# Key units of a paged attention in eight pairs, with a strip of queries for two sequences

## The chip, the cores and the metric

The kernel runs on one core of a Trainium2 chip. The metric is the device time of one execution in microseconds (us), smaller being better. A core has TensorE (PE in the profile; the loads of its stationary operand are listed apart as PEld), VectorE (DVE), ScalarE (ACT), GpSimd (POOL) and SyncE (SP). Each works through its own instructions in their order and waits on semaphores for the others. SP and POOL here also issue DMAs; all DMAs of the core share 16 DMA engines.

## The reference

One decoder layer: a half-step feed-forward block, a token mixer (a gated convolution beside a "forgetting" attention), a second half-step feed-forward block and a gated embedding. It is computed for 256 prompt tokens and for 8 sample sequences of 4 new tokens each, 288 columns in all. The change touches the attention of the sample group alone, whose past lies in pages of 128 rows:

```python
def fox_sample(q, k_new, v_new, logf_new, cache_k, cache_v, cache_logf, page_table):
    DB, T = q.shape[0], q.shape[1]                 # 8 sequences, 4 new tokens
    P = page_table.shape[1] * PAGE_SIZE            # 8 pages of 128 rows
    k_past = cache_k[page_table].reshape(DB, P, N_HEADS, HEAD_DIM)
    ...
    s = jnp.einsum('bqhd,bkhd->bhqk', q, k_all, preferred_element_type=jnp.float32) * SCALE
    s = s + Fq[..., None] - F[:, :, None, :]
    ...
    p = jax.nn.softmax(s, axis=-1)
    return jnp.einsum('bhqk,bkhd->bqhd', p.astype(v_all.dtype), v_all)
```

There are 64 pages of keys and 64 of values, 512 KB each (128 rows x 8 heads x 128 x 4 bytes).

## The kernel before, in words

**Layout.** Activations lie feature by token: 16 tiles of 128 features by 288 tokens. Every weight matrix is cut into chunks of 512 rows by 256 columns (512 KB), loaded by SP into eight slots (`wraw`, L237) and split by ACT and DVE into a high and a low fp32r part (`whi` L276, `wlo` L277, five half-chunks of buffer). A chunk is one step of the program, called a piece below: 2 output blocks x 4 row blocks x 3 matmuls (L313 to L315) = 24 matmuls of 128x128 by 128x288.

**The attention stage.** `pair()` gives lists of such pieces. After the queries' projection the rest of the mixer is one list `fill`: pieces 0 to 15 project the keys, 16 to 51 three of the four convolution groups, and so on. The table `marks` puts other work ahead of chosen pieces, by `at(i, ...)`; `between()` strings both together. So the order of TensorE is: pieces, and ahead of some of them a marked function.

**A key unit.** There are 16 units; unit n holds four pages (half a past) of one sequence. Its keys come by four indirect DMAs that POOL issues (L248) into a tile `KT` of 2 MB, of which there are two. Its scores are 8 matmuls (L688) of 128x32 by 128x512 in plain fp32, four at a time in four column strips of the array; the profile counts each as two, 16 rows in all. The 32 stationary columns are a window on a zeroed `strip` into which DVE copies the four queries of the sequence at columns 28 to 31 (L679); the window's place decides to which rows of the PSUM bank the queries go, so that four units add into one bank. After the fourth, DVE adds the bank to the score tile `s` (L694).

**Order.** Unit n stands ahead of piece 1 + 3n (`KSTEP` = 3): pieces 1, 4, ... 46. The loads of a unit are an item of the same look-ahead list as the weight chunks (`load_upto`, eight items ahead). A KT tile is free when the matmuls of the unit two before it are done; POOL waits for that in its own order. The new tokens' scores (`new_scores`, L703) stand ahead of piece 22, the two softmaxes (`softmax`, L712 to L716) ahead of 27 and 49, the start of the value stage (`v_start`) ahead of 48, and its first round (L746) ahead of 51. POOL also writes the eight key blocks of the result to memory (L614, 144 KB each), as they come out of pieces 0 to 15.

Of the kernel before, what the change touches and what calls it, by code (L numbers as in the profile page):

```python
# [16 lines left out]
F32 = mybir.dt.float32  # L17
# [3 lines left out]
ALU = mybir.AluOpType  # L21
# [4 lines left out]
P = 128  # L26
D = 2048
KT = D // P
# [6 lines left out]
NH = 8  # L35
CB = 8
PAGES = 8
# [7 lines left out]
HALVES = 5  # L45
MANUAL = False
BANKS = dict(mm=3, kt=3, va=2)
KSTEP = 3
WEIGHTS = 4
VPAGES = 3  # L50
AHEAD = 12
# [42 lines left out]
def build(nc, tc, ctx, A, O):  # L94
# [3 lines left out]
    v, s, g, pe, sy = nc.vector, nc.scalar, nc.gpsimd, nc.tensor, nc.sync  # L98
# [8 lines left out]
    def bank(tag, bufs):  # L107
        return ps.tile([P, 512], F32, name=tag, tag=tag, bufs=bufs)
# [15 lines left out]
    h = cst.tile([P, KT, NT], F32, name="h")  # L124
# [11 lines left out]
    at = 0  # L136
# [13 lines left out]
    idx = cst.tile([P, 64], I32, name="idx")  # L150
# [74 lines left out]
    steps = []  # L225
# [3 lines left out]
    def load_upto(n):  # L229
        while state["loaded"] < min(n, len(items)):  # L230
            it = items[state["loaded"]]
            if it["kind"] == "p" and "vx" not in W:
                return
            if it["kind"] == "w":
                state["wslot"] = (state["wslot"] + 1) % (WEIGHTS if state["pages"] and not state["through"] else RAW)
                t = rawp.tile([P, it["nk"], 256], F32, name="wraw", tag=f"raw{state['wslot']}")
                src = it["src"]  # L237
                if state["loaded"] == 0:
                    tc.keep_in_program_order(sy.dma_start(t[:, :2], src[:, :2]))
                    d = sy.dma_start(t[:, 2:], src[:, 2:])  # L240
                else:
                    d = sy.dma_start(t, src)
                if state["used"] < 24:
                    tc.keep_in_program_order(d)
            elif it["kind"] == "k":
                t = W["kt"][0].tile([P, 4, NH, P], F32, name="KT", tag="KT", bufs=2)
                for i, r in enumerate(it["rows"]):
                    g.indirect_dma_start(out=t[:, i].rearrange("p h s -> p (h s)"), out_offset=None, in_=it["src"],  # L248
                                         in_offset=bass.IndirectOffsetOnAxis(ap=r, axis=0))
            else:  # L250
                t = page_tile()
                g.indirect_dma_start(out=t, out_offset=None, in_=it["src"],  # L252
                                     in_offset=bass.IndirectOffsetOnAxis(ap=it["rows"], axis=0))
            it["tile"] = t
            state["loaded"] += 1

    def page_tile():

        own = ([(rawp, f"raw{i}") for i in range(WEIGHTS, RAW)] + [(W["vx"][0], f"v{i}") for i in range(VPAGES)]
               + [(W["mix"][0], "wideb")])  # L260
        n = state["pages"]
# [76 lines left out]
    def do(fn):  # L338
        steps.append(([], fn))
# [3 lines left out]
    def defer(fn, chunks=1):  # L343

        deferred.append((state["chunk"] + chunks, fn))
# [137 lines left out]
    M = {}  # L483
# [156 lines left out]
    def q_gather():  # L640

        kq = W["kq"][0]
        qs = M["qs"] = kq.tile([P, NH, NS], F32, name="qs")
        for hh in range(NH):
            v.tensor_copy(qs[:, hh, :], q[hh][:, SEQ:])
        M["strip"] = kq.tile([P, NH, 60], F32, name="strip")
        g.memset(M["strip"], 0.0)
        M["qn"] = []
        for gi in range(2):
            t = kq.tile([P, NH, 4, 2, DT], F32, name=f"qn{gi}")  # L650
            g.memset(t, 0.0)
            for hh in range(NH):
                v.tensor_copy(t[:, hh, :, hh // 4, :], qs[:, hh, 16 * gi:16 * gi + 16].rearrange("p (b t) -> p b t", t=DT))
            M["qn"].append(t.rearrange("p h b a t -> p h (b a t)"))

    def wide(pool_name, slot, name):
        return W[pool_name][0].tile([P, 9 * P], F32, name=name, tag=f"wide{slot}")

    def fb_load(gi):

        t = wide("mix", "ab"[gi], f"s{gi}")
        for c in range(4):
            off = FS.offset + (gi * 4 * NH + c) * PAGES * P
            g.dma_start(t[32 * c:32 * c + 32, :PAGES * P],
                        bass.AP(tensor=FS.tensor, offset=off,
                                ap=[[NH * PAGES * P, 4], [4 * PAGES * P, 2], [0, DT], [1, PAGES * P]]))
        M["s", gi] = t[:, :PAGES * P + NS]
        x = t[:, :PAGES * P]
        v.tensor_scalar(x, x, -1.0, M["Fq"][gi], ALU.mult, ALU.add)

    def k_scores(n):

        gi, pp, bb = n // 8, n // 4 % 2, n % 4
        seq = 4 * gi + bb
        it = dict(kind="k", src=A["cache_k"], rows=[idx[:, j:j + 1] for j in range(seq * PAGES + 4 * pp, seq * PAGES + 4 * pp + 4)])

        def fn():
            strip = M["strip"]
            v.tensor_copy(strip[:, :, 28:32], M["qs"][:, :, 4 * seq:4 * seq + 4])  # L679
            first, last = bb == 0, bb == 3  # L680
            if first:
                M["sb"] = bank("va", BANKS["va"])
            sb = M["sb"]
            for half in range(2):
                at = 28 - 8 * bb - 4 * half
                for c in range(4):
                    hh = 4 * half + c
                    pe.matmul(sb[32 * c:32 * c + 32, :], strip[:, hh, at:at + 32],  # L688
                              it["tile"][:, :, hh, :],
                              start=first and half == 0, stop=last and half == 1, tile_position=(0, 32 * c))  # L690
            if last:
                def add():
                    x = M["s", gi][:, pp * 512:pp * 512 + 512]
                    v.tensor_tensor(x, sb, x, ALU.add)  # L694

                defer(add, 0)
        return ([it], fn)
# [210 lines left out]
    def kv_start():  # L908
        closed("fp")
        for n in ("zq", "mix", "cv"):  # L910
            opened(n)
        opened("kq", "right")
        q_gather()
        fb_load(0)
        fb_load(1)

# [22 lines left out]
    do(mix_start)  # L939
    qe = qk_evac(q, 0, SCALE, "q")  # L940
    ke = qk_evac(k_, 8, None, "k")
    units = [k_scores(n) for n in range(16)]
    for i in range(4):
        steps.extend(pair(win, 3072 + i * 256, ks, xact, qe(i), **(dict(late=2, tag="va") if i == 0 else {})))
        if i < 2:
            steps.append((units[i][0], lambda: None))
# [14 lines left out]
    def out_conv(ob):  # L961
        def evac(b, o):
            k = 2 * ob + b
            t = W["cv"][0].tile([P, NT], F32, name="tB", tag="tB", bufs=3)
            v.tensor_tensor(t, o, rsc, ALU.mult)
            g.tensor_tensor(h[:, k, :], h[:, k, :], t, ALU.add)
        return evac
# [19 lines left out]
        fill += conv_pair(i)  # L987
    for ob in range(KT // 2):
        fill += pair(A["w_out"], ob * 256, list(range(8)), lambda k: zc[k], out_conv(ob), late=1 if ob == 0 else 0)
    for n in range(16):  # L990
        at(1 + KSTEP * n, units[n] if n > 1 else units[n][1])
    at(22, lambda: new_scores(0), lambda: new_scores(1))
    at(27, lambda: softmax(0))
    at(49, lambda: softmax(1))
    at(48, v_start)
# [152 lines left out]
```

## Time and profile before

| What | Value |
|---|---|
| median of 3 runs (lowest to highest) | 2330.11 us (2329.85 to 2330.43) |
| the profiled execution, its own time | 2329.32 us |
| its span, first to last instruction | 2327.5 us |
| granted TensorE clock | 0.998 |
| PE busy in the key stage, 910.8 to 1088.0 us | 177.2 of 177.2 us |
| DMA share and rate in the key stage | 0.87, 308 GB/s |
| DMA share and rate in the span before it, 0 to 840 us | 0.57, 178 GB/s |
| POOL busy in the key stage | 82.4 us |

The span leaves out about 1.8 us of the execution's time (2329.32 - 2327.5). The profile lists for each engine how long it was busy and, for each group of instructions, how long the engine was idle just before them and what ended that. The chain of waits goes back from the last instruction of the program to what released it, step by step; its rows give the start, the length and the line. A row of a stretch gives its busy time on each engine, the granted clock, the mean busy share of the 16 DMA engines and GB/s. A queue's row gives packets, MB and the share of the 16 engines' time; q0 is the queue of POOL's DMAs, q1 that of SP's.

### The profile page before, as it was taken

The numbers are of one execution on the slowest core, as the hardware profiler recorded it, in microseconds if no ns is written. First come the engines' busy times: TensorE is split into PE (matmuls) and PEld (weight loads), VectorE is DVE, ScalarE is ACT, GpSimd is POOL, SyncE is SP. The second block draws the span as 40 slices with busy tenths as digits, with TensorE's granted clock in tenths as the row PEclk, the third lists the DMA queues.
The fourth block names the chain that finished last, engine by engine and source line by source line (L and its number), as shares of the span: only waits on it lengthen the run. The fifth ranks groups of instructions, "written<-read, shape, count | busy, mean of one in ns | idle before, by whom it ended". The sixth has DMA issues, their size and how long they took to land.

```text
span 2327.5 us, 44281 instructions
## 1 busy us (share of the span) xinstructions
PE 2313.5 (99%) x17385; PEld 2253.7 (97%) x17385; DVE 1342.6 (58%) x2403; ACT 1058.9 (45%) x1865; POOL 330.6 (14%) x403
## 2 busy tenths in 40 slices
PE   9999999999999999999999999999999999999997
PEld 9999999999999999888888999999999999999997
DVE  7555555555555586456466765555555555555755
ACT  7444444444444453334344554444434444444654
POOL 2010000000000013444445210000000000000110
PEclk9999999999999999999999999999999999999999
DMA  8575555555555547987988555555555555555552
GB/s 272 161 242 163 164 168 164 167 163 164 166 167 166 163 159 228 333 314 268 320 317 294 164 165 158 176 154 173 164 167 164 167 163 164 165 167 166 165 166 88
DMA packets 341985, 443.43 MB, mean 191 GB/s; under 512 B 17120, under 2 KB 306288, under 8 KB 341776
## 3 DMA queue, kind: packets, MB, share of 16 engines
q1 hardware_dynamic: 320304, 366.81, 49.6%
q0 software_dynamic: 20384, 71.38, 9.0%
q8 instruction: 136, 2.23, 0.4%
q10 hardware_dynamic: 1088, 2.42, 0.3%
q14 instruction: 73, 0.60, 0.1%
HBM read 435.48 MB, written 5.07 MB: 189 GB/s over the span
## 4 chain that ended last, share of the span: by engine, by line
PE 99%; DVE 0%; ACT 0%; DMA 0%; issue 0%; DVEq 0%
PE mm L313 31%; PE mm L315 31%; PE mm L314 31%; PE va L688 1%; PE va L746 1%; PE va L315 1%; PE va L313 1%; PE va L314 1%; DVE h L1075 0%; PE kt L315 0%; PE kt L313 0%; PE kt L314 0%; DMA gT<-in_gains_dram 0%; PE kt L800 0%; PE kt L833 0%; PE kt L824 0%
## 5 line engine op out<-in xcount | busy, mean ns | idle before, releaser
L277 DVE TENSOR_TENSOR wlo<-wraw,whi 128x512 fp32r<-128x512 f32 x1384 | 973.8, 707 | 802.3 <-ACT whi L276 753.6
L276 ACT ACTIVATE whi<-wraw 128x512 fp32r<-128x512 f32 x1384 | 866.9, 630 | 933.0 <-PE mm L314 903.5
L313 PE MATMUL mm<-xh,whi 128*128 128x288 f32 x3680 | 1094.2, 297 | 0.0
L314 PE MATMUL mm<-xl,whi 128*128 128x288 f32 x3680 | 1085.7, 295 | 0.0
L315 PE MATMUL mm<-xh,wlo 128*128 128x288 f32 x3680 | 1082.0, 294 | 0.0
L313 PEld LDWEIGHTS mm<-xh,whi 128*128 128x128 f32 x3680 | 689.5, 187 | 22.2 <-issue 19.4
L315 PEld LDWEIGHTS mm<-xh,wlo 128*128 128x128 f32 x3680 | 693.0, 188 | 0.1
L314 PEld LDWEIGHTS mm<-xl,whi 128*128 128x128 f32 x3680 | 690.8, 188 | 0.1
L313 PE MATMUL mm<-hh,whi 128*128 128x288 f32 x1408 | 416.8, 296 | 0.0
L314 PE MATMUL mm<-hl,whi 128*128 128x288 f32 x1408 | 415.4, 295 | 0.0
L315 PE MATMUL mm<-hh,wlo 128*128 128x288 f32 x1408 | 414.0, 294 | 0.0
L379 POOL TENSOR_TENSOR sr<-sg,rs 128x288 f32<-128x288 f32 x88 | 72.5, 825 | 1408.9 <-ACT sg L377 1408.8
L315 PEld LDWEIGHTS mm<-hh,wlo 128*128 128x128 f32 x1408 | 265.2, 188 | 0.0
L314 PEld LDWEIGHTS mm<-hl,whi 128*128 128x128 f32 x1408 | 264.3, 188 | 0.0
L313 PEld LDWEIGHTS mm<-hh,whi 128*128 128x128 f32 x1408 | 263.7, 187 | 0.0
L399 DVE SCALAR_TENSOR_TENSOR h<-mm,h 128x288 f32<-128x288 f32 x192 | 87.2, 455 | 23.4 <-PE mm L315 22.9
L220 POOL TENSOR_TENSOR acc<-acc,sq 128x288 f32<-128x288 f32 x59 | 51.3, 870 | 246.9 <-ACT sq L219 244.0
L248 POOL DMA_INDIRECT KT<-in_cache_k_dram,idx x64 | 66.2, 1034 | 128.7 <-PE va L688 55.4
L377 ACT ACTIVATE sg<-tg 128x288 f32<-128x288 f32 x88 | 39.1, 444 | 98.4 <-DVE tg L375 98.3
L386 ACT ACTIVATE hh<-hd 128x288 fp32r<-128x288 f32 x88 | 39.1, 446 | 92.8 <-DVE hd L384 92.8
L252 POOL DMA_INDIRECT page<-in_cache_v_dram,idx x64 | 64.4, 1006 | 72.0 <-PE va L746 50.1
L387 DVE TENSOR_TENSOR hl<-hd,hh 128x288 fp32r<-128x288 f32 x88 | 40.8, 465 | 22.0 <-ACT hh L386 22.0
(233 smaller groups left out, 1323.8 us busy)
## 6 DMA issues: line engine op xcount, KB each, us to landing
wraw<-in_w_ffn_up_dram SPq DMA_DIRECT2D x176, 512.0 KB, 3.6
wraw<-in_w_ffn_gate_dram SPq DMA_DIRECT2D x175, 512.0 KB, 3.6
wraw<-in_w_ffn_down_dram SPq DMA_DIRECT2D x160, 512.0 KB, 3.5
wraw<-in_w_in_dram SPq DMA_DIRECT2D x96, 512.0 KB, 5.2
wraw<-in_w_out_dram SPq DMA_DIRECT2D x32, 512.0 KB, 4.1
wraw<-in_w_ple_gate_dram SPq DMA_DIRECT2D x32, 512.0 KB, 3.7
wraw<-in_w_ffn_down_dram SPq DMA_DIRECT2D x32, 256.0 KB, 3.0
wraw<-in_w_ple_proj_dram SPq DMA_DIRECT2D x8, 256.0 KB, 3.0
```

The costliest lines, as they stand in the source:

```text
L220: (v if k >= KT - last_on_v else g).tensor_tensor(acc, acc, sq, ALU.add)
L248: g.indirect_dma_start(out=t[:, i].rearrange("p h s -> p (h s)"), out_offset=None, in_=it["src"], in_offset=bass.IndirectOffsetOnAxis(ap=r ...
L252: g.indirect_dma_start(out=t, out_offset=None, in_=it["src"], in_offset=bass.IndirectOffsetOnAxis(ap=it["rows"], axis=0))
L276: s.activation(hi, x, AF.Copy)
L277: v.tensor_tensor(lo, x, hi.bitcast(F32), ALU.subtract)
L313: pe.matmul(o, hi[:, j % 2, w], xh, start=f, stop=False)
L314: pe.matmul(o, hi[:, j % 2, w], xl, start=False, stop=False)
L315: pe.matmul(o, lo[:, j % 2, w], xh, start=False, stop=l)
L377: s.activation(u, t, AF.Silu)
L379: g.tensor_tensor(r, u, rs, ALU.mult)
L387: v.tensor_tensor(H["lo"][:, k, :], t, H["hi"][:, k, :].bitcast(F32), ALU.subtract)
L399: v.scalar_tensor_tensor(h[:, k, :], o, 0.5, h[:, k, :], ALU.mult, ALU.add)
```

## The change

The units are taken two by two. Pair m computes units 2m and 2m+1, one behind the other, ahead of piece KPAIRS[m]; right behind it in the program it fills the strip for units 2m+2 and 2m+3 and loads their keys. The loads leave the look-ahead list (the first two units are loaded during the queries' projection, as before). The strip grows from 60 to 92 columns, with the queries of even units at columns 28 to 31 and of odd ones at 60 to 63. The new tokens' scores move from piece 22 to piece 27, behind the fifth pair and ahead of the first softmax. Nothing is added to or left out of the computation.

```diff
-KSTEP = 3
+KPAIRS = (1, 8, 14, 21, 27, 34, 40, 47)
...
-            elif it["kind"] == "k":
-                t = W["kt"][0].tile([P, 4, NH, P], F32, name="KT", tag="KT", bufs=2)
-                for i, r in enumerate(it["rows"]):
-                    g.indirect_dma_start(out=t[:, i].rearrange("p h s -> p (h s)"), out_offset=None, in_=it["src"],
-                                         in_offset=bass.IndirectOffsetOnAxis(ap=r, axis=0))
...
-        M["strip"] = kq.tile([P, NH, 60], F32, name="strip")
+        M["strip"] = kq.tile([P, NH, 92], F32, name="strip")
...
+    def k_load(n):
+
+        t = M["KT", n] = W["kt"][0].tile([P, 4, NH, P], F32, name="KT", tag="KT", bufs=2)
+        seq, pp = 4 * (n // 8) + n % 4, n // 4 % 2
+        for i in range(4):
+            j = seq * PAGES + 4 * pp + i
+            g.indirect_dma_start(out=t[:, i].rearrange("p h s -> p (h s)"), out_offset=None, in_=A["cache_k"],
+                                 in_offset=bass.IndirectOffsetOnAxis(ap=idx[:, j:j + 1], axis=0))
+
+    def k_strip(n):
+        seq = 4 * (n // 8) + n % 4
+        c = 28 + 32 * (n % 2)
+        v.tensor_copy(M["strip"][:, :, c:c + 4], M["qs"][:, :, 4 * seq:4 * seq + 4])
...
     def k_scores(n):
...
-            strip = M["strip"]
-            v.tensor_copy(strip[:, :, 28:32], M["qs"][:, :, 4 * seq:4 * seq + 4])
...
-                at = 28 - 8 * bb - 4 * half
...
+            at = 28 + 32 * (n % 2) - 8 * bb - 4 * half
...
+    def k_pair(m):
+        for n in (2 * m, 2 * m + 1):
+            k_scores(n)
+        for n in (2 * m + 2, 2 * m + 3):
+            if n < 16:
+                k_strip(n)
+                k_load(n)
...
-    for n in range(16):
-        at(1 + KSTEP * n, units[n] if n > 1 else units[n][1])
-    at(22, lambda: new_scores(0), lambda: new_scores(1))
+    for m, i in enumerate(KPAIRS):
+        at(i, lambda m=m: k_pair(m))
+    at(KPAIRS[4], lambda: new_scores(0), lambda: new_scores(1))
```

How this stands on TensorE, at the first unit (ahead of piece 1; `KT` is the tile of keys, `va` the bank of scores; the row's x8 are the unit's 8 matmuls). Before:

```order
L314 MATMUL mm_10812<-xl_9447,whi_10714 128x288
L315 MATMUL mm_10812<-xh_9446,wlo_10715 128x288
L688 MATMUL va_10848<-KT_9915,strip_10777 32x512 x8
L313 MATMUL mm_10811<-xh_9446,whi_10718 128x288
L314 MATMUL mm_10811<-xl_9447,whi_10718 128x288
```

and now (L692 is the changed kernel's line of the same matmul, L308 to L310 those of the pieces):

```order
L309 MATMUL mm_10811<-xl_9447,whi_10714 128x288
L310 MATMUL mm_10811<-xh_9446,wlo_10715 128x288
L692 MATMUL va_10846<-KT_10204,strip_10774 32x512 x8
L692 MATMUL va_10846<-KT_10433,strip_10774 32x512 x8
L308 MATMUL mm_10810<-xh_9446,whi_10718 128x288
L309 MATMUL mm_10810<-xl_9447,whi_10718 128x288
```

Two units stand in a row between the same two pieces, into the same bank.

How it stands on POOL, over the first loads of keys in the stage (`KT`) and the writes of key blocks to memory (`out_1`). Before:

```order
L614 DMA out_1_dram<-k_10960 128x288
L248 DMA KT_10963<-in_cache_k_dram,idx_79 128x1024 x4
L248 DMA KT_11090<-in_cache_k_dram,idx_79 128x1024 x4
L614 DMA out_1_dram<-k_11115 128x288
L614 DMA out_1_dram<-k_11130 128x288
L248 DMA KT_11214<-in_cache_k_dram,idx_79 128x1024 x4
L614 DMA out_1_dram<-k_11274 128x288
```

and now (L672 loads keys, L609 writes them out):

```order
L672 DMA KT_10864<-in_cache_k_dram,idx_79 128x1024 x4
L672 DMA KT_10870<-in_cache_k_dram,idx_79 128x1024 x4
L609 DMA out_1_dram<-k_10963 128x288
L609 DMA out_1_dram<-k_10978 128x288
L609 DMA out_1_dram<-k_11107 128x288
L609 DMA out_1_dram<-k_11122 128x288
L672 DMA KT_11144<-in_cache_k_dram,idx_79 128x1024 x4
L672 DMA KT_11150<-in_cache_k_dram,idx_79 128x1024 x4
```

Eight loads of keys stand together where there were four; four of the writes to memory now lie between the loads that follow the first pair and those that follow the second, two behind the second and two behind the third. The order of SP's loads of weights is the same in both.

More of the change, by code (lines that the diff above doesn't have):

```diff
@@ L671, in k_scores @@
+    def k_strip(n):
+        seq = 4 * (n // 8) + n % 4
+        c = 28 + 32 * (n % 2)
+        v.tensor_copy(M["strip"][:, :, c:c + 4], M["qs"][:, :, 4 * seq:4 * seq + 4])
     def k_scores(n):
         gi, pp, bb = n // 8, n // 4 % 2, n % 4
-        seq = 4 * gi + bb
-        it = dict(kind="k", src=A["cache_k"], rows=[idx[:, j:j + 1] for j in range(seq * PAGES + 4 * pp, seq * PAGES + 4 * pp + 4)])
-        def fn():
-            strip = M["strip"]
-            v.tensor_copy(strip[:, :, 28:32], M["qs"][:, :, 4 * seq:4 * seq + 4])
[L680 to L684, printed above, removed]
-                at = 28 - 8 * bb - 4 * half
[L686 to L696, printed above, removed]
@@ L697, in k_scores @@
-        return ([it], fn)
+        strip, kt = M["strip"], M.pop(("KT", n))
+        first, last = bb == 0, bb == 3
+        if first:
+            M["sb"] = bank("va", BANKS["va"])
+        sb = M["sb"]
+        for half in range(2):
+            at = 28 + 32 * (n % 2) - 8 * bb - 4 * half
+            for c in range(4):
+                hh = 4 * half + c
+                pe.matmul(sb[32 * c:32 * c + 32, :], strip[:, hh, at:at + 32], kt[:, :, hh, :],
+                          start=first and half == 0, stop=last and half == 1, tile_position=(0, 32 * c))
@@ L699, in new_scores, with add @@
+        if last:
+            def add():
+                x = M["s", gi][:, pp * 512:pp * 512 + 512]
+                v.tensor_tensor(x, sb, x, ALU.add)
+            defer(add, 0)
+    def k_pair(m):
[5 more added lines that the diff above has]
+                k_load(n)
     def new_scores(gi):
@@ L913, in kv_start @@
         q_gather()
+        k_strip(0)
+        k_strip(1)
         fb_load(0)
@@ L941, in build @@
     ke = qk_evac(k_, 8, None, "k")
-    units = [k_scores(n) for n in range(16)]
     for i in range(4):
@@ L945, in build @@
         if i < 2:
-            steps.append((units[i][0], lambda: None))
+            do(lambda i=i: k_load(i))
         if i == 0:
```

## The prediction

> **What bounds the kernel now.** I read the page first: who is busy, what the DMA engines do, and the chain that ended last.
>
> ```profile
> PE 2313.5 (99%) x17385; PEld 2253.7 (97%) x17385; DVE 1342.6 (58%) x2403; ACT 1058.9 (45%) x1865; POOL 330.6 (14%) x403
> DMA  8575555555555547987988555555555555555552
> PE 99%; DVE 0%; ACT 0%; DMA 0%; issue 0%; DVEq 0%
> ```
>
> TensorE ends everything: 99% of the chain. Only work that leaves TensorE, or a stall put into it, moves the time. The second row says where a stall could come from: elsewhere the DMA engines are half busy, but in the key stage (slices 15 to 18 of 58 us) they are at 0.7 to 0.9 and more.
>
> Then the chain in the key stage, for the price of a unit:
>
> ```profile
> 920.11 0.14 PE mm L313
> 920.51 0.14 PE mm L313
> ...
> 922.51 1.85 PE va L688 x16
> 924.36 0.33 PE mm L313
> ...
> 934.16 1.85 PE va L688 x16
> 936.01 0.33 PE mm L313
> ```
>
> L313 is every third matmul of a piece and comes each 0.40 us, so a matmul takes 0.133 us and a piece of 24 takes 3.20 us. From unit to unit are 11.65 us (934.16 - 922.51), with three pieces in it (9.60), so a unit costs 2.05 us.
>
> The loads of the stationary operand show what these 2.05 us are made of:
>
> ```profile
> 922.09 0.19 PEld L315 LDWEIGHTS mm<-xh,wlo 128*128 128x128 f32 x1
> 922.44 0.16 PEld L688 LDWEIGHTS va<-KT,strip 128*32 128x32 f32 x8 [0.17 <-issue]
> 922.90 0.13 PEld L688 LDWEIGHTS va<-KT,strip 128*32 128x32 f32 x4 [0.30 <-issue]
> 923.33 0.13 PEld L688 LDWEIGHTS va<-KT,strip 128*32 128x32 f32 x4 [0.30 <-issue]
> 924.29 0.19 PEld L313 LDWEIGHTS mm<-xh,whi 128*128 128x128 f32 x1 [0.84 <-issue]
> ```
>
> Sixteen loads are four rounds of four strips, and rounds follow each other at 0.43 us (923.33 - 922.90): 1.72 us of streaming. The other 0.33 us (2.05 - 1.72) is paid on the way in and out: 0.35 us from the last load of a piece to the first of the unit instead of 0.133, and a first L313 of 0.33 us in the chain instead of 0.14.
>
> **What the change removes.** Units 2m and 2m+1 now stand in a row. If the way in and out is paid once a pair, a pair costs 8 x 0.43 + 0.33 = 3.77 us instead of 4.10, and eight pairs save 8 x 0.33 = **2.6 us**. Bounds: the 0.33 us on L313 is 0.19 above its neighbours and surely goes once (8 x 0.19 = 1.5 us); more than 2.7 us (rounds of 0.427, 1.85 / 4 less the way in) is not in the chain. I take 2.6, since the rounds inside a unit already follow without a gap. Nothing else on TensorE is removed or added: 256 rows of the same matmul stay.
>
> **What it adds: keys in one burst.** Now the waits of TensorE and SP in this stage, and the loads.
>
> ```profile
> PEld va L688 <- issue: 11.9, 46, 0.3
> PEld mm L313 <- issue: 10.9, 13, 0.8
> PEld va L688 <- DMA KT<-in_cache_k_dram,idx: 0.3, 2, 0.2
> SPq L242 <- DVE wlo L277: 169.5, 45, 17.6
> DMA to landing us min/median/max: 4.1/6.2/9.7
> 910.86 1.85 PE va L688 x16
> 913.03 1.05 POOL L248 DMA_INDIRECT KT<-in_cache_k_dram,idx  x1 [20.27 <-PE va L688]
> 914.39 0.99 POOL L248 DMA_INDIRECT KT<-in_cache_k_dram,idx  x1 [0.30 <-issue]
> 915.68 0.95 POOL L248 DMA_INDIRECT KT<-in_cache_k_dram,idx  x1 [0.30 <-issue]
> 916.93 1.26 POOL L248 DMA_INDIRECT KT<-in_cache_k_dram,idx  x1 [0.30 <-issue]
> 924.67 1.01 POOL L248 DMA_INDIRECT KT<-in_cache_k_dram,idx  x1 [0.47 <-PE va L688]
> ```
>
> Today no unit waits for its keys: 0.3 us in all. A load is issued 0.3 us after the unit whose tile it takes (912.71, then 913.03), four go out at 1.3 us each, and the last lands some 6.2 us after 916.93, about 923.1. The unit that uses it starts at 934.16: 11 us to spare.
>
> In pairs both tiles come free within one pair. Count from a pair's start. The first tile is free at 1.85 us, the eight issues run from 2.2 to about 12.5 us, and both tiles are due at the next pair: with six pieces between (three of the seven gaps) the first at 3.77 + 6 x 3.20 = 23.0 and the second, behind one unit, at 24.8 us; with seven pieces (four gaps) at 26.2 and 28.0. By the landing row alone the last lands near 11.2 + 6.2 = 17.4, with 7 us to spare. But that row is of four loads; eight are 4.19 MB, and the DMA engines must carry them beside the weights.
>
> ```profile
> 914.80:919.20 4.40, 4.40 (x35) 4.40 (x35) 1.50 (x3) 1.90 (x3) 2.79 (x3) 1.00 0.94 290
> 945.00:950.00 5.00, 5.00 (x41) 3.40 (x40) 2.17 (x4) 1.17 (x2) 1.73 (x2) 1.00 0.99 392
> 914.80:1076.00 161.20, 161.20 (x1251) 138.96 (x1250) 79.69 (x149) 59.09 (x98) 76.61 (x88) 1.00 0.91 322
> q0 software_dynamic: 340, 1.26, 92.4%
> q0 software_dynamic: 8481, 30.69, 55.8%
> q1 hardware_dynamic: 5760, 20.97, 34.8%
> out_dram<-k POOLq DMA_DIRECT2D x8, 144.0 KB, 6.0
> ```
>
> The last three columns of a stretch are clock, DMA share and GB/s; the q0 and q1 rows are MB of POOL's and SP's queues, the first q0 row in 914.8 to 919.2, the others in 914.8 to 1076. POOL's keys move from 914.8 on, 1.8 us after the first issue, at 290 GB/s while they are alone. Over the stage the engines moved 322 GB/s at a share of 0.91, that is 354 at a share of 1, and in one mixed stretch 392.
>
> In pairs the keys move from 4.0 us on, so in a gap of six they have 24.8 - 4.0 = 20.8 us. SP waits only for splits to free a slot, so weights come at the pieces' pace: six chunks in 23.0 us, some 5.4 (2.83 MB) in these 20.8. Together 7.02 MB, which takes 19.8 us at 354 GB/s (on time) and 21.8 at 322 (1.0 us late). In a gap of seven, 4.19 + 3.36 MB = 7.55 MB in 24.0 us are 23.4 us even at 322. The key blocks written to memory (0.147 MB each) add four to the first gap, two to the second and two to the third; at 322 these gaps are then 1.3, 1.9 and 0.3 us late. Sum of stalls: 0 us at 354, 5.5 us at 322 (1.3 + 1.9 + 0.3, and 1.0 in each of the other two gaps of six). With eight loads queued the engines have work through the whole burst, which is nearer to the first end, so I take a quarter: **1.4 us**.
>
> The page "DMA: Bandwidth & Descriptors" of the Trainium skill (Specifications) gives about 358 GB/s as what HBM grants one core. By that, an estimate, the gap of six needs 19.6 us, and no stall is left; the 392 above is over that figure, so the measurement decides.
>
> **Edits costed at nothing.** (a) The strip's copies: DVE waited for the unit before each; now two wait for the pair, with splits behind them. Five half-chunks are split ahead, and TensorE uses none during a pair; without this cover it would be a wait of a few tenths a pair. (b) The new scores move beside the first softmax. DVE's chain there:
>
> ```profile
> 995.32 1.25 DVE L712 TENSOR_REDUCE nm<-s 128x1 f32<-128x1056 f32 x1
> 996.60 1.18 ACT L713 ACTIVATE s<-s,nm 128x1056 f32<-128x1056 f32 x1 [3.67 <-DVE nm L712]
> 998.78 1.29 DVE L277 TENSOR_TENSOR wlo<-wraw,whi 128x512 fp32r<-128x512 f32 x2
> ```
>
> From the reduction to the next split done are 4.1 us (995.32 to about 999.4). Begun near 4.8 us after the fifth pair's start, with one more evacuation ahead, that split is ready at about 9.4; TensorE needs it after the pair, the new scores, two pieces and a quarter, near 11.3. If it slipped, the stall is 1 or 2 us, once. (c) POOL spends 10 us in a row issuing; what stands behind (a product for the convolution, the blocks' writes) is used pieces later, and ACT's splits go on until then. (d) The last pair stands one piece later than the last unit did; values start by freed weight slots, and their first round is four pieces on.
>
> **Sum.** 2329.32 (the profiled execution; span 2327.5 and 1.8 around it) - 2.6 + 1.4 = 2328.1. That execution is 0.8 us under the median of the runs, so **2328.9 us** as a median: 0.05% faster, which nobody can tell from no change. The bound of what can be told is about 0.2%, 4.7 us here: faster is below 2325.4, slower above 2334.8.
>
> **Rivals.** (1) *Given back*: keys are late in most gaps by 1 or 2 us, 3 to 7 us in all. For it: the keys got 30.69 MB in 161.2 us, 190 GB/s, and a gap of six asks for 201. Against: that mean has POOL idle from landing to the next issue (923.1 to 924.67 of 11.65 us). Time, with the 5.5 us of the sum: 2330.1 - 2.6 + 5.5 = 2333.0.
>
> (2) *Slower*: under a lasting backlog the keys get only half of what the engines move, 161 of 322 GB/s. Then 4.19 MB take 26.0 us, the second tile is 5.2 us late in the three gaps of six and 2.0 in the four of seven, 23.6 us: 2330.1 - 2.6 + 23.6 = 2351. It decides the sign from about 180 GB/s down (three gaps 2.5 us late, 7.4 in all). For it: in 945 to 950, with both queues at work, the engines were full. Against: weights ask for no more than 164 GB/s (0.524 MB a piece), nothing during a pair, and the rest is the keys'. The page "DMA: Bandwidth & Descriptors" of the Trainium skill (Queues, rings and completion order) says that an engine takes turns between its queues, which is this rival's rule; no run here shows yet how long both stay full.
>
> (3) *Way in and out paid for each unit*, only the 1.5 us saved: 2330.1 - 1.5 + 1.4 = 2330.0. Against it: the rounds' even step.
>
> (4) *More is saved*: if all idle time of the loads before L688 and behind it (11.9 + 10.9 us) were time of TensorE, half of it would go, 11.4 us: 2318.7. Against: the chain has only 0.33 us of it per unit; the rest lies under streaming matmuls.
>
> **Chances.** Forecast (stalls under 3 us) 0.60, given back 0.18, slower 0.13, paid for each unit 0.05, more saved 0.04. So faster 0.04, same 0.60 + 0.18 + 0.05 = 0.83, slower 0.13. The range 2327.0 to 2334.5 holds the full saving without a stall (2327.5) with 0.5 us of scatter (the runs spread over 0.6), and the first rival with 1.5 us more; it leaves out (2), (4) and little else. The forecast's own range is 2327.0 to 2330.8.
>
> **What would show it.** Right: the chain has eight stretches of 32 rows of the score matmul of about 3.6 us each instead of sixteen of 1.85, one L313 of 0.33 behind each; the wait of these loads for the DMA of the keys stays under 3 us in all and falls on the first two gaps and those of six; DMA share over 0.9 inside a gap. Wrong: stretches of 3.9 us (rival 3), a wait for keys over 7 us (rival 2), or a wait for a split behind the fifth pair (edit b).

## The result, and the profile after

In the recorded comparison the changed kernel took 2342.16 us (median of 6 runs, 2341.21 to 2344.18) against 2329.98 us before (6 runs, 2329.81 to 2330.43, three of them those of the table ahead of the prediction): a ratio of 1.0053, 95% interval 1.0042 to 1.0063, 12.2 us slower. The profiled execution took 2341.21 us, its span is 2339.4 us; before, the span was 2327.5.

That is not the whole result. The same kernel ran four more times, each time beside the kernel before on one chip, and took 2326.7 to 2327.3 us on all three chips that it came to (table below), a ratio of 0.9985 to 0.9990. The forecast of 2328.9 us missed the recorded comparison by 13 us and these four by about 2. So two questions stand: where the 12 us went where they were lost, and why they are lost in one place and not in another.

First the trace of the recorded comparison. The page, after the change (busy us by engine, the DMA row of the 40 slices, the chain by engine):

```profile
PE 2315.4 (99%) x17385; PEld 2255.7 (96%) x17385; DVE 1340.6 (57%) x2403; ACT 1057.6 (45%) x1865; POOL 332.2 (14%) x403
DMA  8575555555555447878888454545555455555552
PE 98%; DVE 1%; ACT 0%; another core or an unknown queue 0%; DMA 0%; issue 0%; SPq 0%; DVEq 0%
```

The chain has lost 1% of TensorE, and in the key stage (slices 16 to 19) the DMA row has 7, 8, 7, 8 where before it had 7, 9, 8, 7: the stage takes longer for the same bytes (287 GB/s from the first pair to the eighth, 308 over the stage before). The pairs themselves are what the forecast said. The chain at the first pair (start, us, what):

```profile
911.16 3.57 PE va L692 x32
914.73 0.33 PE mm L308
```

One stretch of 32 rows, one L308 of 0.33 us behind it. Now the stage cut from pair to pair, in the changed kernel of the recorded comparison (columns: length, then busy us and count of TensorE, its weight loads, VectorE, ScalarE and GpSimd, then granted clock, DMA share, GB/s):

```profile
911.09:938.64 27.55, 26.89 (x201) 23.46 (x200) 10.97 (x20) 8.53 (x15) 9.43 (x11) 1.00 0.82 298
990.09:1014.56 24.47, 23.68 (x177) 20.27 (x176) 11.77 (x28) 8.14 (x15) 10.76 (x12) 1.00 0.82 288
1014.56:1047.83 33.27, 29.01 (x233) 25.34 (x233) 15.85 (x28) 11.54 (x21) 13.55 (x15) 0.95 0.72 248
sum 188.15, PE 179.21 PEld 156.32 DVE 85.92 ACT 62.62 POOL 83.72; mean PE 25.60 PEld 22.33 DVE 12.27 ACT 8.95 POOL 11.96
```

and the same cuts of the same kernel in the run f1 below, on chip 8:

```profile
910.84:937.00 26.16, 26.16 (x201) 23.37 (x200) 11.23 (x20) 8.85 (x15) 9.65 (x11) 1.00 0.87 316
986.14:1009.10 22.96, 22.96 (x177) 20.16 (x176) 12.11 (x28) 8.47 (x15) 9.79 (x12) 1.00 0.88 317
1009.10:1035.56 26.46, 26.46 (x234) 23.86 (x233) 15.56 (x28) 11.32 (x21) 13.88 (x15) 1.00 0.85 303
sum 173.85, PE 173.85 PEld 154.48 DVE 86.17 ACT 64.04 POOL 81.21; mean PE 24.84 PEld 22.07 DVE 12.31 ACT 9.15 POOL 11.60
```

From the first pair to the eighth the recorded run needs 188.15 us, the other 173.85, with the same instructions: 14.3 us. Six of the seven gaps lose 0.8 to 1.5 us each (27.55 against 26.16 in the first), the fifth loses 6.8 (33.27 against 26.46). TensorE is without a gap in f1; in the recorded run it stood idle for 8.94 us (188.15 - 179.21). The other 5.4 us (179.21 - 173.85) count as busy: some 1.7 are a slower clock (below), and much of the rest is the start of each pause, since a row's modelled end lies 0.29 us behind its start while the next matmul normally starts after 0.13.

What TensorE waited for there is not the keys. The waits of the recorded run from 900 to 1100 us (who, for whom: us in all, times, longest):

```profile
DVE wlo L272 <- ACT whi L271: 65.9, 36, 6.1
ACT whi L271 <- PE mm L310: 26.1, 8, 6.2
PEld va L692 <- issue: 14.2, 51, 0.3
ACT s L723 <- DMA KT<-in_cache_k_dram,idx: 11.7, 1, 11.7
DVE s L715 <- remote: 4.1, 1, 4.1
```

No row of the score matmul (L692) names the keys' DMA, and its longest wait is 0.3 us, as before the change; every key was there in time. But ScalarE, which splits the weights, once stood for 6.2 us. Its rows behind the first pair, first in the recorded run, then in f1:

```profile
917.23 0.63 ACT L271 ACTIVATE whi<-wraw 128x512 fp32r<-128x512 f32 x1 [5.54 <-issue]
918.03 0.64 ACT L271 ACTIVATE whi<-wraw 128x512 fp32r<-128x512 f32 x1 [0.17 <-PE mm L309]
924.86 2.20 ACT L271 ACTIVATE whi<-wraw 128x512 fp32r<-128x512 f32 x4 [6.20 <-PE mm L310]
```

```profile
916.98 0.63 ACT L271 ACTIVATE whi<-wraw 128x512 fp32r<-128x512 f32 x1 [5.54 <-PE mm L309]
917.78 0.64 ACT L271 ACTIVATE whi<-wraw 128x512 fp32r<-128x512 f32 x1 [0.17 <-PE mm L309]
920.18 0.63 ACT L271 ACTIVATE whi<-wraw 128x512 fp32r<-128x512 f32 x1 [1.76 <-PE mm L309]
920.98 0.64 ACT L271 ACTIVATE whi<-wraw 128x512 fp32r<-128x512 f32 x1 [0.17 <-PE mm L309]
```

In f1 two splits come each 3.20 us, as TensorE uses up a chunk and says so. In the recorded run the pair due at about 920.4 doesn't come; at 924.86 four come at once. TensorE's own rows ran on from the pair's end to 923.46, so the matmuls that free the buffers were done some 4 us before ScalarE went on. The semaphore updates in the trace agree: TensorE's semaphore has none from 918.34 to 924.84 and nine from there to 925.50, where f1 has nine spread over 920.16 to 924.29. The chain there:

```profile
923.46 0.13 PE mm L309
923.59 1.28 PE mm L310
924.88 0.63 ACT whi L271
...
926.74 0.46 DVE k L604
927.20 0.04 issue
927.25 0.40 PE mm L308
```

Here is the 1.4 us of the first gap. TensorE itself falters at 923.59, at matmuls for which the trace names no wait, and again at 927.25 behind a VectorE that is late in turn.

Behind the fifth pair, where new scores and first softmax stand beside each other in this program, the same thing costs more (VectorE and the chain of the recorded run):

```profile
1021.07 0.25 DVE L715 SCALAR_TENSOR_TENSOR s<-kt,fq,nbias 128x32 f32<-128x32 f32 x1 [2.62 <-PE mm L310]
1025.45 0.25 DVE L715 SCALAR_TENSOR_TENSOR s<-kt,fq,nbias 128x32 f32<-128x32 f32 x1 [4.12 <-remote]
1025.61 1.24 DVE L722 TENSOR_REDUCE nm<-s 128x1 f32<-128x1056 f32 x1
```

```profile
1018.20 0.29 PE kt L713 x30
...
1021.32 4.10 another core or an unknown queue
```

In f1 both ran as one row, right behind the scores:

```profile
1012.97 0.62 DVE L715 SCALAR_TENSOR_TENSOR s<-kt,fq,nbias 128x32 f32<-128x32 f32 x2
```

Both L715 need only the new scores (L713), whose matmuls ended at 1018.5 in the recorded run; there one started 2.6 us later, the other 6.9. The reduction, ScalarE's exponential at 1026.89 and the splits behind it in ScalarE's order follow from that. (The row above that puts the exponential's 11.7 us down to the keys' DMA misleads: that DMA is only the last thing that landed. The reduction ended at 1026.85.) TensorE meanwhile trickled, and then its clock fell:

```profile
1020.00:1028.00 8.00, 4.14 (x26) 3.54 (x25) 1.66 (x3) 1.11 (x2) 5.02 (x6) 1.00 0.88 314
1028.00:1032.00 4.00, 3.60 (x16) 3.13 (x15) 3.60 (x6) 2.08 (x6) 2.76 (x4) 0.57 0.77 309
```

26 matmuls in 8 us instead of 60 (8 / 0.133), and then 4 us at a granted clock of 0.57, which by an estimate costs 1.7 us more (4 x 0.43). The page "TensorE: Matmul & The Clock Gate" of the Trainium skill (What's actually happening) says that the clock is halved after an idle window of some 3.4 us. Here the clock fell without such a stop: TensorE's longest idle time in those 8 us is 1.4 us, and it was busy for 4.14 of them.

So in the recorded run, what passes between the engines (a buffer is free, a sum is ready) arrives some us late while GpSimd issues its eight loads and shortly behind: ScalarE and VectorE show it, and TensorE stops also where the trace names no wait. No view shows why.

One thing sets this trace apart beside its times. Its page gives no time from issue to landing for any load; the page of the kernel before does. The same line of both pages, the recorded run's first:

```profile
wraw<-in_w_ffn_up_dram SPq DMA_DIRECT2D x176, 512.0 KB
wraw<-in_w_ffn_up_dram SPq DMA_DIRECT2D x176, 512.0 KB, 3.6
```

The first trace holds 13557 semaphore updates from DMAs, that of f1, the same program, 14405: some of the events are missing from it. Of the runs below, e1 to e4 (chip 7) lack these times too, whether they stall or not, and all runs on chips 8, 2 and 5 have them. So the recorded run and chip 7 share a mark that isn't the program's, and in these traces the event that a row names as the end of a wait is less certain than the start times.

### The profile page after: what moved, and what is told of

The parts are those of the page before. It is cut to its first block, busy times and chain, and to the rows that moved or that the text cites. A ratio compares the mean times of both kernels' runs of the same rounds, so it can differ in the third digit from the quotient of the medians.

```text
span 2339.4 us, 44276 instructions
## 1 busy us (share of the span) xinstructions
PE 2315.4 (99%) x17385; PEld 2255.7 (96%) x17385; DVE 1340.6 (57%) x2403; ACT 1057.6 (45%) x1865; POOL 332.2 (14%) x403
## 4 chain that ended last, share of the span: by engine, by line
PE 98%; DVE 1%; ACT 0%; another core or an unknown queue 0%; DMA 0%; issue 0%; SPq 0%; DVEq 0%
PE mm L308 31%; PE mm L310 30%; PE mm L309 30%; PE va L756 1%; PE va L692 1%; PE va L308 1%; PE va L310 1%; PE va L309 1%; DMA h<-in_x_dram 0%; DVE h L1086 0%; PE kt L308 0%; PE kt L310 0%; PE kt L309 0%; PE kt L810 0%
## 5 line engine op out<-in xcount | busy, mean ns | idle before, releaser
L308 PE MATMUL mm<-xh,whi 128*128 128x288 f32 x3680 | 1094.8, 297 | 4.8 <-issue 2.5
L310 PE MATMUL mm<-xh,wlo 128*128 128x288 f32 x3680 | 1082.8, 294 | 2.6 <-issue 2.5
L308 PEld LDWEIGHTS mm<-xh,whi 128*128 128x128 f32 x3680 | 690.2, 188 | 22.8 <-issue 16.5
L310 PEld LDWEIGHTS mm<-xh,wlo 128*128 128x128 f32 x3680 | 693.3, 188 | 4.5 <-issue 4.4
L308 PE MATMUL mm<-hh,whi 128*128 128x288 f32 x1408 | 416.8, 296 | 0.0
L310 PE MATMUL mm<-hh,wlo 128*128 128x288 f32 x1408 | 414.0, 294 | 0.0
L310 PEld LDWEIGHTS mm<-hh,wlo 128*128 128x128 f32 x1408 | 265.1, 188 | 0.0
L308 PEld LDWEIGHTS mm<-hh,whi 128*128 128x128 f32 x1408 | 263.8, 187 | 0.0
L672 POOL DMA_INDIRECT KT<-in_cache_k_dram,idx x64 | 63.2, 987 | 110.8 <-DVE idx L158 52.8
```

Of the source, the lines that this page charges most:

```text
L308: pe.matmul(o, hi[:, j % 2, w], xh, start=f, stop=False)
L310: pe.matmul(o, lo[:, j % 2, w], xh, start=False, stop=l)
```

## The experiments

All groups; each run from e1 on stands beside the kernel before on its chip (us, medians; ratios with 95% intervals):

| run | chip | this | before | ratio |
|---|---|---|---|---|
| recorded comparison | not named | 2342.16 | 2329.98 | 1.0053 [1.0042, 1.0063] |
| e1 two fours | 7 | 2337.93 | 2330.45 | 1.0034 [1.0020, 1.0048] |
| e2 plain loads | 7 | 2337.30 | 2330.45 | 1.0030 [1.0018, 1.0043] |
| e3 softmax at 24 | 7 | 2340.14 | 2330.45 | 1.0043 [1.0026, 1.0060] |
| e4 no loads | 7 | 2327.54 | 2330.45 | 0.9987 [0.9978, 0.9997] |
| e5 plain from third unit | 8 | 2326.80 | 2329.74 | 0.9988 [0.9978, 0.9997] |
| e6 two fours, softmax at 26 | 8 | 2327.76 | 2329.74 | 0.9990 [0.9981, 0.9999] |
| e7 softmax at 26 | 8 | 2327.07 | 2329.74 | 0.9989 [0.9979, 0.9998] |
| e8 before, half loads | 8 | 2353.53 | 2329.74 | 1.0096 [1.0080, 1.0111] |
| f1 changed kernel | 8 | 2327.10 | 2329.58 | 0.9990 [0.9980, 0.9999] |
| f2 as e7 | 8 | 2327.30 | 2329.58 | 0.9990 [0.9980, 0.9999] |
| f3 as e3 | 8 | 2327.24 | 2329.58 | 0.9990 [0.9980, 1.0000] |
| f4 as e1 | 8 | 2334.32 | 2329.58 | 1.0020 [1.0010, 1.0029] |
| g1 changed kernel | 2 | 2327.03 | 2329.92 | 0.9988 [0.9978, 0.9997] |
| g2 as e6 | 2 | 2327.31 | 2329.92 | 0.9988 [0.9979, 0.9998] |
| h1 changed kernel | 5 | 2326.74 | 2329.79 | 0.9985 [0.9976, 0.9995] |
| h2 as e6 | 5 | 2327.22 | 2329.79 | 0.9989 [0.9979, 0.9998] |
| i1 changed kernel | 5 | 2327.26 | 2329.61 | 0.9989 [0.9979, 0.9999] |
| i2 as e6 | 5 | 2327.52 | 2329.61 | 0.9992 [0.9982, 1.0001] |

**First group (chip 7): which part of the change stalls.** The saving alone, without the loads:

```diff
-        t = M["KT", n] = W["kt"][0].tile([P, 4, NH, P], F32, name="KT", tag="KT", bufs=2)
+        t = M["KT", n] = M["KT0", n % 2] = W["kt"][0].tile([P, 4, NH, P], F32, name="KT", tag="KT", bufs=2)
...
             if n < 16:
                 k_strip(n)
-                k_load(n)
+                M["KT", n] = M["KT0", n % 2]
```

> The changed kernel without the loads of key units 2 to 15: all pairs read the first two units' keys (the scores of the later units are left wrong by that). It shows the saving and the edits on VectorE and TensorE alone. Theories A and B: no stall, 8 x 0.33 us saved: 2327.5 us. If the stalls come from the strip copies or from another order of instructions (theory C among them): 2333 to 2342.

2327.54 us, 2.9 below the kernel before. The pairs, the two-column strip and the moved scores cost nothing and save what was said; the whole loss hangs on the loads.

The same loads as plain ones, of fixed pages instead of those of the table, so that the scores are of other keys:

```diff
-            g.indirect_dma_start(out=t[:, i].rearrange("p h s -> p (h s)"), out_offset=None, in_=A["cache_k"],
-                                 in_offset=bass.IndirectOffsetOnAxis(ap=idx[:, j:j + 1], axis=0))
+            g.dma_start(t[:, i].rearrange("p h s -> p (h s)"), A["cache_k"][j * P:j * P + P, :])
```

> [...] Theory B (the burst of transfers starves the weights): the bytes and their burst are the same, so the stalls stay: 2338 or more. Theory C: 2333 or more.

2337.30 us, but the trace puts the loss elsewhere. The chain at the kernel's start, and the stage from the first pair to the eighth (e2):

```profile
20.63 10.89 DMA wraw<-in_w_ffn_gate_dram
```

```profile
sum 173.86, PE 173.86 PEld 154.46 DVE 86.04 ACT 64.53 POOL 56.26; mean PE 173.86 PEld 154.46 DVE 86.04 ACT 64.53 POOL 56.26
```

In this program plain loads wait for no table, so the first two units' went out from 1.3 us on and held up the first weights: the first pair starts 10 us later than in f1 (920.98 against 910.84). The key stage is free of stalls: 173.86 us, as without loads. Here 4.19 MB also come in one burst behind each pair, beside the weights. That speaks against theory B of e1: a burst of transfers alone doesn't starve the splits. GpSimd's part is shorter, a median of 0.54 us for an issue against 0.95 for an indirect one. Both kinds go by the same queue, q0 software_dynamic (4.49 MB from 920 to 947 us here, as much in the recorded run from 911 to 938), so the queue as such isn't what stalls. That agrees with the page "DMA: Bandwidth & Descriptors" of the Trainium skill (SWDGE vs HWDGE vs iDMA), by which GpSimd's loads, direct and indirect, take the software path.

The softmax away from the fifth pair:

```diff
-    at(KPAIRS[4], lambda: new_scores(0), lambda: new_scores(1))
-    at(27, lambda: softmax(0))
+    at(23, lambda: new_scores(0), lambda: new_scores(1))
+    at(24, lambda: softmax(0))
```

> The changed kernel with the new scores ahead of piece 23 and the first softmax ahead of piece 24, away from the fifth pair's burst at 27. Theories A and C: behind the fifth pair only the 1.5 us of the other pairs is left instead of 6.8, so about 2336.8 us, and no stall of the softmax at 24, which is behind the fourth pair's loads by then. Theory B: the transfers are as before, 2341 to 2343.

2340.14 us. The large stall moved with the softmax (e3, third to sixth pair):

```profile
962.51:989.98 27.47, 26.42 (x201) 23.39 (x200) 11.33 (x21) 8.53 (x15) 10.85 (x12) 1.00 0.85 299
989.98:1019.48 29.50, 26.89 (x209) 23.38 (x208) 14.25 (x33) 9.51 (x17) 10.48 (x12) 0.88 0.70 239
1019.48:1045.65 26.17, 26.17 (x202) 23.37 (x201) 13.74 (x23) 10.16 (x19) 15.15 (x15) 1.00 0.88 315
```

and the gap with the softmax in the same kernel as f3, on chip 8:

```profile
986.09:1009.63 23.54, 23.54 (x209) 20.54 (x208) 14.14 (x33) 9.51 (x17) 10.79 (x12) 1.00 0.82 298
```

The gap with the softmax loses 6.0 us (29.50 - 23.54), the fifth gap nothing at all. So a burst of eight doesn't always stall, and where a chain across VectorE and ScalarE stands behind one, it stalls most. Behind the first pair ScalarE's rows nearly repeat the recorded run's (splits at 917.23 and 918.38, then four at 924.85).

Two bursts of four:

```diff
+        M["held"] = kt
...
             if n < 16:
                 k_strip(n)
-                k_load(n)
+        if m < 7:
+            k_load(2 * m + 2)
+
+    def k_second(m):
+        it, j = halves[state["split"] - 1]
+        x = cst.tile([1, 1], F32, name="held", tag="held")
+        v.tensor_tensor(x, M["held"][:1, 0, 0, :1], it["parts"][j][1][:1, 0, :1].bitcast(F32), ALU.add)
+        k_load(2 * m + 3)
...
+    for m, i in enumerate(KPAIRS[:-1]):
+        at(i + 3, lambda m=m: k_second(m))
```

> The second unit's four loads are held back until the split of about three pieces later (a one-element read of its tile on VectorE keeps the tile taken), so that POOL never issues more than four key loads in a row; all else as changed. Theory A (POOL issuing eight indirect loads in a row holds up the signals that TensorE, ScalarE and VectorE pass each other): the idle ScalarE behind each pair goes, all stalls go, the 2.6 us of saving stay: 2327.5 us, 0.999 of before. Theory B (the keys' transfers starve the weights, and the splits wait for weights): the same, 2327.5. Theory C (the order at the fifth pair, new scores and first softmax beside each other, is the main loss): the 1.4 us at the other pairs may go, about 5.4 stay: 2333.

2337.93 us. From the first pair to the fifth, then the fifth gap, then the last two (e1, and below it the same kernel as f4 on chip 8):

```profile
910.72:1008.98 98.26, 98.26 (x753) 87.09 (x752) 45.89 (x89) 33.79 (x55) 39.42 (x46) 1.00 0.90 317
1008.98:1037.34 28.36, 27.35 (x234) 23.95 (x233) 15.57 (x29) 11.10 (x21) 13.52 (x15) 1.00 0.78 274
1037.34:1092.68 55.34, 51.14 (x378) 44.07 (x377) 27.10 (x52) 18.95 (x33) 27.53 (x32) 0.97 0.81 274
```

```profile
910.98:1009.46 98.48, 98.47 (x753) 87.06 (x752) 45.75 (x89) 33.81 (x55) 40.01 (x46) 1.00 0.89 316
1009.46:1035.91 26.45, 26.45 (x233) 23.83 (x232) 16.46 (x29) 11.43 (x21) 14.03 (x15) 1.00 0.87 316
1035.91:1091.24 55.33, 50.92 (x377) 43.70 (x376) 27.10 (x52) 18.96 (x33) 27.52 (x32) 0.97 0.78 266
```

With four loads in a row the first four gaps have no stall on chip 7 (98.26 us, as in f1), where e3 lost 1.4, 0.9 and 1.3 in the three ahead of its softmax. The fifth, with the softmax, still loses 1.9 (28.36 - 26.45). The last two lose 6.2 on both chips (55.33 - 49.13): there the held-back loads came too late, and the score matmul waits 4.4 us for keys in f4. That part is the experiment's own fault.

**Second group (chip 8): more of the same questions, on another chip.** Plain loads from the third unit on:

```diff
-            g.indirect_dma_start(out=t[:, i].rearrange("p h s -> p (h s)"), out_offset=None, in_=A["cache_k"],
-                                 in_offset=bass.IndirectOffsetOnAxis(ap=idx[:, j:j + 1], axis=0))
+            if n < 2:
+                g.indirect_dma_start(out=t[:, i].rearrange("p h s -> p (h s)"), out_offset=None, in_=A["cache_k"],
+                                     in_offset=bass.IndirectOffsetOnAxis(ap=idx[:, j:j + 1], axis=0))
+            else:
+                g.dma_start(t[:, i].rearrange("p h s -> p (h s)"), A["cache_k"][j * P:j * P + P, :])
```

> As the plain loads before, but the first two units keep their indirect loads, so that nothing of the keys is loaded at the kernel's start (units 2 to 15 read fixed pages). If eight plain loads in a row cost the key stage nothing, as the trace of the run before reads, and its 10 us were lost at the start: 2327.5 us (2327.0 to 2328.5). If the transfers' burst costs something after all: above 2332.

2326.80 us: the 10 us of e2 were the start's.

For e6, the diff of e1 with two pieces instead of three (`at(i + 2`), and with the edit of e7, which is the following alone:

```diff
-    at(KPAIRS[4], lambda: new_scores(0), lambda: new_scores(1))
-    at(27, lambda: softmax(0))
+    at(25, lambda: new_scores(0), lambda: new_scores(1))
+    at(26, lambda: softmax(0))
```

> Pairs with the second unit's four loads held back to the split of about two pieces later (one piece earlier than in the first trial, where the keys came late behind the fifth and sixth pair), new scores ahead of piece 25 and first softmax ahead of 26. Theory A (five or more indirect loads in a row hold up the engines' signals): no stall, the saving stays: 2327.5 to 2328.5 us, faster than before by some 0.1%. If any burst of four between pairs also stalls, or keys are late: 2330 to 2334.

> The changed kernel with its bursts of eight, new scores ahead of piece 25 and first softmax ahead of piece 26: six pieces after the fourth pair's loads began and before the fifth's begin. If the fifth pair is worse only because new scores and softmax wait for signals that are late in a burst: all bursts cost about 1.4 us, 2336 to 2337. If the fifth pair is worse for another reason: 2342.

2327.76 and 2327.07 us. (The third pair of e6, and of f2 below, loses 0.3 us: the operand's load for its second unit waits 1.0 us instead of 0.3.) The second was the surprise: bursts of eight, and no stall anywhere, although up to the 24th piece its instructions are those of the changed kernel, in the same order with the same waits. Neither theory A nor C allows that.

The kernel before with its loads halved:

```diff
-                    g.indirect_dma_start(out=t[:, i].rearrange("p h s -> p (h s)"), out_offset=None, in_=it["src"],
-                                         in_offset=bass.IndirectOffsetOnAxis(ap=r, axis=0))
+                    for a in (0, 64):
+                        g.indirect_dma_start(out=t[a:a + 64, i].rearrange("p h s -> p (h s)"), out_offset=None, in_=it["src"],
+                                             in_offset=bass.IndirectOffsetOnAxis(ap=r[:64], axis=0))
```

> The kernel before, each of its loads issued as two of 64 rows (the second half of the rows taken from the same indices as the first, so the scores are of other keys): eight indirect loads in a row behind every unit, the same bytes, 2 MB a burst as before. If the number of issues in a row, or the 10 us that POOL spends on them, is what holds up the signals: stalls behind the units, 2340 to 2355 us. If it is the rows or bytes that stand queued (1024 rows of 4 KB behind a pair, 512 here): no stall, 2330.

2353.53 us, but it doesn't answer its question. An issue of 64 rows takes as long as one of 128 (0.90 against 0.96 us), GpSimd waited 24.4 us in all for earlier loads, a load landed 10.1 us behind its issue (median; 6.2 before), and TensorE waited for keys. With the same bytes in twice the issues the keys come late; of signals it shows nothing.

**Third group (chip 8 again): the program or the place.** No edit; four kernels from above.

> The changed kernel once more, on one chip with the next three, since up to the fifth pair its instructions are those of the run with the softmax at 26, which had no stall at any pair, while it had one behind the first. If the stalls belong to this program: 2342 us, with a stall behind every pair. If they belong to the chip that ran it (the first four trials ran on one chip, the next four on another): all four of this group alike, either all with stalls behind the first pair or none.

> The softmax at 26 with bursts of eight again. Stalls of the program: 2327 as before. Stalls of the chip: about 2337 if the changed kernel here takes 2342, and 2327 if that takes 2332 or less.

> The softmax at 24 again. Stalls of the program: 2340. Stalls of the chip: 2340 where the changed kernel takes 2342, else 2327 to 2328.

> Two bursts of four, softmax left at 27, again. Stalls of the program: 2338. Stalls of the chip: 2338 where the changed kernel takes 2342; else only what late keys cost, 2327 to 2332.

2327.10, 2327.30, 2327.24 and 2334.32 us. The changed kernel has no stall here, and neither has the kernel of e3, which lost 12 us on chip 7. So the stalls don't belong to the program alone.

**Fourth to sixth group (chips 2, 5 and 5).** The changed kernel and e6 side by side, in the hope of a place that stalls.

> The changed kernel a third time, on whatever chip comes. If the stalls belong to the chip: either 2326.5 to 2328 with no gap in the matmuls behind the pairs, as in the group before, or 2340 to 2344 with the gaps of the first trace, and nothing between. If they come and go on one chip: a time between, or runs of both kinds here.

> Two bursts of four with the softmax at 26, beside the changed kernel. Where that stalls: this one shows whether bursts of four are enough to avoid it (2327.5 to 2329) or not (2331 to 2338). Where it doesn't: 2327.5, the same as before.

> The changed kernel a fourth time, on whatever chip comes: 2326.5 to 2328 without gaps behind the pairs, or 2340 to 2344 with them. Two chips of three that are known by now had none.

> Two bursts of four with the softmax at 26 beside it. On a chip that stalls: 2327.5 to 2329 if bursts of four with a pause avoid the stalls, 2331 to 2338 if not. Elsewhere 2327.5.

> The changed kernel a fifth time, on whatever chip comes: 2326.5 to 2328 without gaps behind the pairs, or 2340 to 2344 with them. Three chips of four that are known by now had none.

> Two bursts of four with the softmax at 26 beside it. On a chip that stalls: 2327.5 to 2329 if bursts of four with a pause avoid the stalls, 2331 to 2338 if not. Elsewhere 2327.5.

2327.03 and 2327.31, 2326.74 and 2327.22, 2327.26 and 2327.52 us: no stall. Within each group the two kernels differ by no more than 0.5 us.

**What is settled and what stays open.** Shown: without loads, and with plain ones, the stage has no stall even on chip 7; with bursts of four indirect loads it has none there in the first four gaps; with bursts of eight it stalls in the recorded comparison and on chip 7, and not on chips 8, 2 and 5; moving the softmax moves the largest stall. Not shown: that the chip is the cause and not the hour, since chip 7 didn't come again and the chip of the recorded comparison isn't named; why signals are late there; and whether e6 avoids the stalls on a chip that has them. It was never run on one. Two rivals for the reason stand untested. An engine that stops without a wait could lack its next instructions; the trace doesn't speak for it, as the packets of the instruction queue (q8) took a median of 1.07 us in this stage of the recorded run and 0.99 in f1, but when they were asked for can't be seen. And since events are missing from just these traces, the recording of events could itself hold up the engines there; every execution on record has a recorded span, so none tells the two apart.

## Why the prediction was right and wrong

**The saving** was right. 8 x 0.33 = 2.6 us was the sum; the span went from 2327.5 to 2324.9 us in f1, 2.6, and e4's ratio is 0.9987. Rounds stay at 0.43 us, and the way in and out is paid once a pair. Rivals 3 and 4 fall with that.

**Late keys**, 1.4 us (0 to 5.5), came out at 0: in no trace of the changed kernel does TensorE stand before a score matmul (a load of its operand waits 0.2 us for a DMA, once, in f1 and g1). In f2, with the same loads, the third pair's second unit starts 0.3 us late. The lower end, from 354 GB/s, was the right one: in f1 a gap of six took 22.96 us, its pieces and pair and nothing else. Rival 2 named the right sign for the recorded comparison with the wrong place; its keys were in time.

**Edits (a) and (b)**, the strip's copies and the new scores beside the softmax, were rightly costed at nothing wherever signals come in time: f1 and f3 have no gap, with the softmax at 27 or 24, and f2 (at 26) loses 0.3 us. In the recorded run the stall stood where the prediction looked for a sign against it, behind the fifth pair, and not only there. (b) is where 6.8 us went, against the "1 or 2 us, once" of the text. But it wasn't the wait for a split that the text had in mind. ScalarE's splits did stand still for 13.3 us (from 1015.2 to 1028.5); TensorE, though, began to falter at 1020.4, some 15 matmuls behind the new scores, when the five half-chunks of edit (a) would have held for up to 60.

**The step that failed is edit (c)**: "POOL spends 10 us in a row issuing; what stands behind ... is used pieces later, and ACT's splits go on until then." It looked at what waits behind GpSimd in its own order, and priced that at nothing. In the recorded run ACT's splits did not go on: from 918.03 to 924.86 there is none, and 14.3 us are lost in seven gaps. The trace of before had four issues in a row and no stall, and the prediction took eight for twice the same without a bound for it; no rival had it, and the range, built from the keys alone, ended 8 us short. On the other three chips the step holds. Why the bursts stop the engines on one chip and not on the others stays open.

So where the stalls are, 14.3 us less the 2.6 saved make about 12; elsewhere nothing is taken from the 2.6. The forecast is some 2 us high there, 1.4 of them for keys that weren't late.

## What to carry to other kernels

A burst of indirect loads can cost more than the time of its transfers: where three engines hand each other buffers every few us, keep it no longer than what a trace has shown to be harmless, or leave pauses in it. Bursts of four with a pause (e6, g2, h2, i2) took 0.3 to 0.7 us more than the bursts of eight beside them (e7, g1, h1, i1); on the chip that stalls, fours (e1) removed the loss from four gaps and left 1.9 us in the one with the softmax (in the last two its own late keys hide the answer). A loss of half a per cent that no view explains should be seen on a second chip before the program is blamed or changed. And of a wait for several things, the one that a view names is only the one that came last: compare its time with the start of what waited (11.7 us "for the keys" were a wait for VectorE).

## What the hardware did that was not expected

The same instructions took 188.15 us between the first and the last pair in the recorded run, and 173.85 in f1; the median of the kernel before stayed within 2329.6 to 2330.5 us in all groups. Chip 7 has the highest, by 0.5 us, which is less than its runs scatter (2329.57 to 2331.85), so its times don't tell a chip that stalls from one that doesn't. In the recorded run TensorE falters where the trace names no wait (923.59, and 26 matmuls in 8 us from 1020), while ScalarE and VectorE start up to 7 us after what they need is done. An indirect load of 64 rows costs GpSimd 0.90 us and one of 128 rows 0.96, a plain one 0.54.
